# Four adaLN rows formed by GpSimd beside the latent attention, and a sixth early chunk pair in layer 0

## The chip, the cores and the metric

The kernel runs on one core of a Trainium2 chip. The metric is the device time of one execution in microseconds. Five engines work side by side, each with its own queue that is executed in order: TensorE (PE, matrix products), VectorE (DVE), ScalarE (ACT), GpSimd (POOL) and SyncE (SP, which here issues the transfers). An instruction that waits holds up everything behind it on its engine.

## The reference

A trunk of two layers on one sequence of 1024 tokens of width 1024, in float32. Each layer has a mixer of three head groups and a gated feed-forward part, and both are modulated by adaLN from a condition vector c:

```python
c_act = jax.nn.silu(c)
for l in range(DEPTH):
    mod = (c_act @ ada_w[l] + ada_b[l])[:, None, :]
    sh1, sc1, g1, sh2, sc2, g2 = jnp.split(mod, N_MOD, axis=-1)
    h = rms_norm(x, norm1_w[l]) * (1.0 + sc1) + sh1
    ...
    y = concat(window_attention(h), latent_attention(h), spatial_gating(h))   # shortened
    x = x + g1 * (group_norms(y) @ w_out[l])                                  # shortened
    h = rms_norm(x, norm2_w[l]) * (1.0 + sc2) + sh2
    x = x + g2 * ((silu(h @ w_gate) * (h @ w_up)) @ w_down[l])                # shortened
```

The six pieces of `mod` are the adaLN rows. In the kernel a row is named (layer, j), with j from 0 (sh1) to 5 (g2). Row (l, j) is the sum over 1024 entries of silu(c) times a row of 1024 columns of `ada_w`.

## The kernel before

**Stages.** Each layer runs as: projection of the input, window attention and spatial gating (layer 0 about 74 to 330 us of the profiled span, layer 1 1228 to 1500), latent attention with the output projection, which runs beside its second half (330 to 531, 1503 to 1706), the gate/up products (531 to 987, 1706 to 2142), and the down products (987 to 1205, 2141 to 2354).

**Precision and the product scheme.** Every float32 operand of a product is split into a high and a low part (`split`, L142 to L143 and L140: ACT casts the high part, DVE subtracts it from the operand to give the low one), and three products replace one (`mm3`, L134 to L137). The gate/up and down products are done in a seven-product scheme over pairs of chunks: `left` and `right` form sums of quarter blocks (L1435: POOL or DVE), each sum is split, and `gu_pair` (L1482) or the down stage multiplies them. There are 11 chunk pairs (NJ = 11) of seven steps each.

**adaLN rows.** A row is formed away from PE: the weights come in eight blocks of 128x1024 (the tile `ada`), and `ada_mac` (L253) multiplies block k by column k of `cact` (silu(c) as columns) and adds it to `acc`, all on DVE: L255 for the first block, L257 for the other seven. When all eight are in, `ada_reduce` (L401) transposes `acc` on PE, four blocks of 128x128 to one PSUM bank (L404, the tile `adaT`), and DVE sums the bank along its free dimension (L405, the tile `mc`); a whole row needs two such banks. `ada_finish` (L382) adds the bias and, for the rows that are needed along the free dimension, transposes and stores them to DRAM, from where `mod_row` (L473) loads them broadcast as `mrow`.

Three places make rows. `ada_rows_wide` (L407) runs as the step B of the order strings PRU0 and PRU1 in the projection stage, with two blocks at a step: rows (0,2), (0,4), (0,3) in layer 0 and (1,4), (1,3) in layer 1. `ada_bg` (L443) runs within the gate/up stage of layer 0, one block at a call, for the rows (0,5), (1,1), (1,0), (1,2) and (1,5). The first two rows of layer 0 are made at the start of the program, which the change doesn't touch.

**Early pairs.** `wd_early` (L1565) is run from within the gate/up stage: for each chunk pair j in EARLY[l] it loads two down-weight tiles (`dnr`, 128x1024), waits three steps, multiplies them by the gate row (L1575: one on DVE, one on POOL, with the row (l,5) as `mrow`), forms the seven right-hand sums, splits each (the tile `wpe`) and keeps it for a store to DRAM (`wp`). In the down stage such a pair's seven operands are loaded (`dnt<-wp`) and not formed. EARLY0[l] is the number of steps that pass first. Layer 0 has five early pairs and begins after 14 steps, layer 1 six and begins after one.

**What sets the order.** The kernel is written as generators, and strings of letters give the order of their steps: PRU0 and PRU1 in the projection stages, PRB0 and PRB1 in the latent attention, a letter for each generator (S the softmax, T and H the transposes of probabilities and heads, M the products with the values, O the output tiles, and so on; `sequences`, L197). In the gate/up stage `pair_steps` (L1697) calls `ahead(i)` before step i of a pair j > 0: it runs one step of `bg` (a multiply-add) if 7(j-1)+i < 9 or i < 4, then one step of `bg2` (the early pairs). Since an engine executes in program order, the place of a step in these strings is its place in each engine's queue.

**Names for the steps below.** `QK` holds queries and keys of one of eight sequence tiles; the rotation (L360 to L363, on POOL) is its last change, the copy L844 the one before; `qkTB` (L1160) are PE's transposes of them at the start of the latent attention, and `mB` (L1133, L1134) its mask. `pB`, `nmB` (L1177) are the masked scores and their negated maxima, `pTs` the split transposed probabilities. `ks`, `qs`, `kw`, `pLA`, `yA` belong to the window attention, `yc` to the spatial gating, `wor` to the output weights. Small tiles of 128x512 come from `AD` (L150), a pool of NAD = 4 buffers.

Of the kernel before, what the change touches and what calls it, by code (L numbers as in the profile page):

```python
# [12 lines left out]
ALU = mybir.AluOpType  # L13
AX = mybir.AxisListType

P = 128
# [37 lines left out]
DY1, DY2 = 0, 0  # L54
PRU0 = ("fKKRKKfKRKQKQSSKSKPPRBQVVRfKSPSSQLKKPRSPVVKPQVSPVKKSRPSLQVVKPSRPcSQcLRVVPLPQhShLcSSSVPVecczcVPPB"
       "hcPVVLVculuuxqzBBxLlueBxqoeuuLoeoqyosouuqlqylxxyxyysllohyBylsqxoqxyyBxxleyyxByyxyxyxooBysqxx")
PRU1 = ("fKfKKKfKRRKQKSSKQKPSPRSQVVSSKRKQLKPRPSPVVRPVKQoQSSSPVKKPVRSLBPVLKSQPVBcPcVRSQLBPeLVhcPhBSScVzSccB"
        "PVPcVhVVPBLcuuluozBxlLxeyquByquLxxllBoqouuuqosBeyllhoyyByllxxeyxBxqoyxxyyBoyxqxsyysBxqysxxeyyxqo")
PRB0 = ("HHHHSHHSSSHTTSTSTHTSTMMMMSTMHMTMSHTTMHSMMTTTMHTMMSMMMSTTSqHMSTMTHMTSqTMHTSMTMMMSMHTHTMTMTMMgTHMT"
       "MMSSSSTHSTMMHTwMqTTTMSMSMSTqTMTMHTTTMSMMHTMMMTSMSyxTSaMqSTTxHHMMSqxwMMSySxTSSTHyMHwSTMMSMyqTTMSM"  # L60
       "THaMOSSHTHMSHMqMMTTMSSqOSSTMqwMTTTMqSMMSSxwOMTyMyTyxxOMwOOqOnOnwOynbnbwOjbxObrnhOnkbhrsOssntttbt"
       "OtObbOtn")
PRB1 = ("HHHHSHHSSSHTTSTSTHTSTMMMMSTMHMTMSHTTMHSMMTTTMHTMMSMMMSTTSqHMSTMTHMTSqTMHTSMTMMMSMHTHTMTMTMMgTHMT"
       "MMSSSSTHSTMMHTwMqTTTMSMSMSTqTMTMHTTTMSMMHTMMMTSMSyxTSaMqSTTxHHMMSqxwMMSySxTSSTHyMHwSTMMSMyqTTMSM"
       "THaMOSSHTHMSHMqMMTTMSSqOSSTMqwMTTTMqSMMSSxwOMTyMyTyxxOMwOOqOnOnwOynbnbwOjbxObrnhOnkbhrsOssntttbt"
       "OtObbOtn")
EY = (1, 0, 1, 1, 0, 0, 0, 1)
ORD = ((0, 1, 2, 3, 4, 6, 5), (0, 2, 3, 1, 4, 6, 5))
AHEAD = (4, 2, 6, 10, 7, 9, 9)
EARLY = ((0, 1, 3, 5, 8), (0, 1, 3, 5, 6, 8))  # L70
EARLY0 = (14, 1)
NG = 33
NW = 12
NR = 4
# [5 lines left out]
def tile_trunk(ctx, tc, x, c, positions, ada_w, ada_b, norm1_w, w_in, a_sinks, b_q_norm_w, b_w_uq,  # L80
# [326 lines left out]
    def ada_rows_wide(l, js):  # L407
# [32 lines left out]
            yield  # L440
        drain(tail)

    def ada_bg(todo):  # L443

        steps = [(l, j, k) for l, j in todo for k in range(KD)]

        def load(l, j, k):
            raw = W([P, D], F32, "ada")
            DMA.dma_start(out=raw, in_=ada_w[l, k * P:(k + 1) * P, j * D:(j + 1) * D])
            return raw  # L450

        def finish(acc, mc, l, j):
            yield
            ada_reduce(acc[:, 0:512], mc[:, 0:4])
            ada_reduce(acc[:, 512:1024], mc[:, 4:8])
            yield from ada_finish(l, j, mc, 2)

        raw, tail = load(*steps[0]), iter(())
        for i, (l, j, k) in enumerate(steps):
            if k == 0:  # L460
                acc, mc = W([P, D], F32, "acc"), TN(8, "mc")
            cur = raw
            if i + 1 < len(steps):
                raw = load(*steps[i + 1])
            ada_mac(acc, cur, k)
            run(tail)
            yield
            if k == KD - 1:
                tail = finish(acc, mc, l, j)
        while run(tail):  # L470
            yield
# [82 lines left out]
    def layer(l, x_tiles):  # L554
# [5 lines left out]
        rs_kv = cst.tile([P, 8], F32, name=f"rskv{l}")  # L560
        rs_a = cst.tile([P, 8], F32, name=f"rsa{l}")
        rs_b = cst.tile([P, 8], F32, name=f"rsb{l}")
        bg = ada_rows_wide(l, (2, 4, 3) if l == 0 else (4, 3))


        w1, g1 = load_in_chunk(l, 512, 512, 2)
# [1099 lines left out]
        def build_t_seq():  # L1666
            need("b", 8)
            need("h", 2)
            b11, b12, b21, b22 = hb[0, 1], hb[0, 0], hb[1, 1], hb[1, 0]
            t2 = [G([P, 2, 512], F32, "t2") for _ in range(2)]  # L1670
            tt2(t2, b22, b12, ALU.subtract)
            yield
            split_h("t3", t2)
            yield
            tt2(t2, t2, b11, ALU.add)
            split_h("t2", t2)
            yield
# [12 lines left out]

        def prep_gu_seq():
            need("j", 1)
            for n in range(2):
                ready.append(next(gens[0]))
                yield

        def pair_steps(j):  # L1697
            def ahead(i):
                if j > 0:
                    if 7 * (j - 1) + i < 9 or i < 4:  # L1700
                        run(bg)
                    run(bg2)
                if i == 3 and j + 1 < NJ:
                    gens[j + 1] = gu_prep(load_gu(j + 1), ORD[1])
                want_gu(7 * j + (AHEAD[i] if j or i > 1 else 2))
            return gu_pair(j, lambda i: ready[7 * j + i], ahead)
# [10 lines left out]
        def pair_seq():  # L1717
            need("r", 2)
            yield from first_products(pair_steps(0), 6)

        seqs = dict(H=heads_seq(), S=soft_seq(), T=t_seq(), M=m_seq(), q=sq_seq(), a=ya_seq(), y=y_seq(), w=w_seq(),
                    g=g_seq(), x=x_seq(), O=o_seq(), k=mods_seq(), n=norm_seq(), b=hb_seq(), h=split_h_seq(),
                    t=build_t_seq(), j=load_gu_seq(), r=prep_gu_seq(), s=pair_seq())
        step, need = sequences(seqs)
        for k in (PRB0, PRB1)[l]:
            step(k)
        for k in seqs:
            need(k, 99)

        bg = ada_bg([(0, 5)] + [(1, j) for j in (1, 0, 2, 5)]) if l == 0 else iter(())  # L1730
        bg2 = wd_early()
        for j in range(1, NJ):
            g = pair_steps(j)
# [65 lines left out]
```

## Time and profile before

| | us |
|---|---|
| median of three runs | 2364.41 |
| lowest, highest | 2363.06, 2368.47 |
| the profiled execution's own time | 2363.91 |
| its span on the core | 2362.2 |
| mean granted clock of TensorE in it | 0.984 |

A row of a group gives line, engine, operation, what is written and read, shape and count, then the time busy in us with the mean of one in ns, then the engine's idle time just before and what ended it. A row of the timeline gives the start in us, the duration, and in square brackets how long the engine had been idle and what released it; "x8" in it joins neighbours of one kind. In a list of one tile's instructions stand the least, the median and the greatest duration in ns. PEld is the load of weights into the PE array, which overlaps the products.

### The profile page before, as it was taken

Reading aid. Unit: us, or ns where it says so; the run is one execution under the profiler, and the core shown is the slowest. Engines: PE = TensorE matmul, PEld = TensorE weight load, DVE = VectorE, ACT = ScalarE, POOL = GpSimd, SP = SyncE. Lnnn points to the kernel's source line nnn. Section 1 sums busy time; section 2 is a strip of 40 time slices with the busy share of each in tenths; the row PEclk is TensorE's granted clock in tenths of the full one; section 3 lists DMA queues with packets and bytes.
Section 4 is the critical chain, followed back from the end, with each engine's and each line's share of the span. In section 5 each row is a group of like instructions: output and inputs, shape, how many; then the busy total and the mean of one; then the engine's idle time right before and its main releaser. Section 6 shows DMA issues by size and latency. Waiting matters only on the chain. (4 is left out here: it accounts for less than half of the span.)

```text
span 2362.2 us, 31945 instructions
## 1 busy us (share of the span) xinstructions
PE 2253.7 (95%) x11191; PEld 1903.5 (81%) x11191; DVE 1783.3 (75%) x2793; ACT 1114.9 (47%) x2296; POOL 981.3 (42%) x997
## 2 busy tenths in 40 slices
PE   5899899999999999999999898999989999999998
PEld 4789798887888877878878787988878888888886
DVE  7787578848778777699974875688597676748978
ACT  4566377637334343323343653785464444432233
POOL 4666640322433323555554655202234243325643
PEclk9999999999999999999999999999999999999999
DMA  6503442212557465863240153222134545468433
GB/s 255 167 19 106 172 139 84 96 54 90 178 195 250 163 222 181 345 256 94 82 158 22 54 181 143 75 88 99 54 102 163 186 156 177 172 230 322 133 109 115
DMA packets 155397, 347.66 MB, mean 147 GB/s; under 512 B 12522, under 2 KB 71652, under 8 KB 155236
## 3 DMA queue, kind: packets, MB, share of 16 engines
q1 hardware_dynamic: 155236, 345.62, 41.9%
q8 instruction: 88, 1.44, 0.2%
q14 instruction: 73, 0.60, 0.1%
HBM read 250.65 MB, written 94.92 MB: 146 GB/s over the span
## 5 line engine op out<-in xcount | busy, mean ns | idle before, releaser
L140 DVE TENSOR_TENSOR gus<-gur,gus 128x512 fp32r<-128x512 f32 x264 | 230.8, 888 | 113.9 <-ACT gus L143 109.0
L135 PE MATMUL gate<-hTh,gus 128*128 128x512 f32 x616 | 244.2, 396 | 17.3 <-ACT u L1530 9.2
L143 ACT CAST gus<-gur 128x512 fp32r<-128x512 f32 x264 | 160.3, 624 | 197.0 <-DVE acc L257 53.4
L135 PE MATMUL down<-dnt,dns 128*128 128x512 f32 x616 | 240.9, 391 | 8.1 <-ACT dnt L143 6.8
L136 PE MATMUL gate<-hTl,gus 128*128 128x512 f32 x616 | 243.0, 394 | 0.6 <-DVE hTl L140 0.5
L137 PE MATMUL gate<-hTh,gus 128*128 128x512 f32 x616 | 242.4, 393 | 0.0
L135 PE MATMUL up<-hTh,gus 128*128 128x512 f32 x616 | 240.5, 390 | 1.6 <-ACT u L1530 1.6
L137 PE MATMUL down<-dnt,dns 128*128 128x512 f32 x616 | 240.0, 390 | 0.0
L136 PE MATMUL down<-dnt,dns 128*128 128x512 f32 x616 | 240.0, 390 | 0.0
L137 PE MATMUL up<-hTh,gus 128*128 128x512 f32 x616 | 239.9, 390 | 0.0
L136 PE MATMUL up<-hTl,gus 128*128 128x512 f32 x616 | 239.9, 389 | 0.0
L143 ACT CAST dns<-act 128x512 fp32r<-128x512 f32 x132 | 81.4, 621 | 234.4 <-PE down L137 178.2
L1435 POOL TENSOR_TENSOR gur<-gur 128x512 f32<-128x512 f32 x44 | 62.6, 1422 | 278.6 <-DVE gus L140 278.6
L1616 DVE TENSOR_TENSOR x<-x,down 128x512 f32<-128x512 f32 x224 | 147.5, 678 | 26.7 <-PE down L137 26.3
L135 PEld LDWEIGHTS gate<-hTh,gus 128*128 128x128 f32 x616 | 117.5, 191 | 43.6 <-ACT u L1530 10.0
L140 DVE TENSOR_TENSOR dns<-act,dns 128x512 fp32r<-128x512 f32 x132 | 136.3, 1050 | 13.0 <-ACT dns L143 13.0
L135 PEld LDWEIGHTS down<-dnt,dns 128*128 128x128 f32 x616 | 115.7, 188 | 35.5 <-ACT dnt L143 5.2
L1435 POOL TENSOR_TENSOR gur<-gur,s 128x512 f32<-128x512 f32 x44 | 67.5, 1540 | 181.1 <-DVE gus L140 181.1
L136 PEld LDWEIGHTS gate<-hTl,gus 128*128 128x128 f32 x616 | 117.5, 191 | 25.7 <-DVE hTl L140 1.7
L137 PEld LDWEIGHTS gate<-hTh,gus 128*128 128x128 f32 x616 | 117.2, 190 | 24.4
L135 PEld LDWEIGHTS up<-hTh,gus 128*128 128x128 f32 x616 | 115.8, 188 | 25.7 <-ACT u L1530 2.0
L136 PEld LDWEIGHTS up<-hTl,gus 128*128 128x128 f32 x616 | 115.7, 188 | 24.0
(417 smaller groups left out, 6209.5 us busy)
## 6 DMA issues: line engine op xcount, KB each, us to landing
gur<-in_w_gate_up_dram SPq DMA_DIRECT2D x88, 512.0 KB
ada<-in_ada_w_dram SPq DMA_DIRECT2D x80, 512.0 KB
wp<-wpe SPq DMA_DIRECT2D x77, 512.0 KB
dnt<-wp SPq DMA_DIRECT2D x77, 512.0 KB
dnr<-in_w_down_dram SPq DMA_DIRECT2D x44, 512.0 KB
act<-act SPq DMA_DIRECT2D x44, 512.0 KB
wr<-in_w_in_dram SPq DMA_DIRECT2D x24, 512.0 KB
x<-in_x_dram SPq DMA_DIRECT2D x16, 512.0 KB
```

The lines of the kernel that those rows point to most:

```text
L135: PE.matmul(ps, lh, rh, start=start, stop=False, skip_group_check=more)
L136: PE.matmul(ps, lh, rl, start=False, stop=False, skip_group_check=more)
L137: PE.matmul(ps, ll, rh, start=False, stop=stop, skip_group_check=more)
L140: eng.tensor_tensor(out=out_, in0=a, in1=b, op=ALU.subtract)
L143: ACT.copy(out=h, in_=src)
L1435: return lambda o, a, b, op: eng.tensor_tensor(out=o, in0=a, in1=b, op=op)
L1616: DVE.tensor_tensor(out=av_, in0=av_, in1=ps[t], op=ALU.add)
```

## The change

The rows (0,5), (1,1), (1,4) and (1,3) leave DVE and are formed on POOL during the latent attention: (0,5) and (1,1) in layer 0's, which were in the gate/up stage behind it, and (1,4) and (1,3) in layer 1's, which were in layer 1's projection. A new generator, `ada_half_rows`, makes each row in two halves of 512 columns. For each half there are eight loads of 128x512 (256 KB), eight multiplies by a column of `cact` and seven additions, as separate POOL instructions since the fused form of L257 is not used there; the half's `ada_reduce` then needs one PSUM bank. It is the step A in PRB0 and PRB1, 40 letters between the seventh and the 181st of the string. The 14 letters B of PRU1 go. In the gate/up stage of layer 0, `bg` keeps the rows (1,0), (1,2) and (1,5), and runs only at steps i < 4.

Chunk pair 6 joins the early pairs of layer 0, so that both layers have the pairs 0, 1, 3, 5, 6 and 8; layer 0's early work begins after three steps and not after 14. That is possible since the row (0,5), by which the down weights are multiplied, is then done before the stage begins.

By instruction counts: DVE loses 32 multiply-adds of 128x1024; POOL gains 64 multiplies and 56 additions of 128x512; SP issues 64 loads of 256 KB in place of 32 of 512 KB, and seven more stores and loads of `wp`. The seven right-hand operands of pair 6 move from the down stage (where POOL forms the sums and ACT and DVE split them) to the gate/up stage (where DVE forms the sums). PE's instructions are the same in number and kind.

```diff
-PRU1 = ("fKfKKKfKRRKQKSSKQKPSPRSQVVSSKRKQLKPRPSPVVRPVKQoQSSSPVKKPVRSLBPVLKSQPVBcPcVRSQLBPeLVhcPhBSScVzSccB"
+PRU1 = ("fKfKKKfKRRKQKSSKQKPSPRSQVVSSKRKQLKPRPSPVVRPVKQoQSSSPVKKPVRSLPVLKSQPVcPcVRSQLPeLVhcPhSScVzSccPVPcV"
...
-PRB0 = ("HHHHSHHSSSHTTSTSTHTSTMMMMSTMHMTMSHTTMHSMMTTTMHTMMSMMMSTTSqHMSTMTHMTSqTMHTSMTMMMSMHTHTMTMTMMgTHMT"
+PRB0 = ("HHHHSHAHSSASHTTASTSATHTSATMMAMMSTAMHMATMSHATTMAHSMMATTTAMHTMAMSMAMMSTATSqAHMSTAMTHAMTSqATMHATSMTA"
...
+PROWS = ([(0, 5), (1, 1)], [(1, 4), (1, 3)])
+GROWS = [(1, j) for j in (0, 2, 5)]
-EARLY = ((0, 1, 3, 5, 8), (0, 1, 3, 5, 6, 8))
-EARLY0 = (14, 1)
+EARLY = ((0, 1, 3, 5, 6, 8), (0, 1, 3, 5, 6, 8))
+EARLY0 = (3, 1)
...
+    def ada_half_rows(todo):
+
+        steps = [(l, j, hf, k) for l, j in todo for hf in range(2) for k in range(KD)]
+
+        def load(l, j, hf, k):
+            raw = AD("ada")
+            DMA.dma_start(out=raw, in_=ada_w[l, k * P:(k + 1) * P, j * D + hf * 512:j * D + hf * 512 + 512])
+            return raw
+
+        raw, tail = load(*steps[0]), iter(())
+        yield
+        for i, (l, j, hf, k) in enumerate(steps):
+            if k == 0:
+                acc = AD("acc")
+                mc = TN(8, "mc") if hf == 0 else mc
+            cur = raw
+            if i + 1 < len(steps):
+                raw = load(*steps[i + 1])
+            col = cact[:, k:k + 1]
+            if k == 0:
+                POOL.tensor_scalar(out=acc, in0=cur, scalar1=col, scalar2=None, op0=ALU.mult)
+            else:
+                POOL.tensor_scalar(out=cur, in0=cur, scalar1=col, scalar2=None, op0=ALU.mult)
+                POOL.tensor_tensor(out=acc, in0=acc, in1=cur, op=ALU.add)
+            run(tail)
+            yield
+            if k == KD - 1:
+                def finish(acc, mc, l, j, hf):
+                    yield
+                    ada_reduce(acc, mc[:, 4 * hf:4 * hf + 4])
+                    yield
+                    if hf:
+                        yield from ada_finish(l, j, mc, 2)
...
-        bg = ada_rows_wide(l, (2, 4, 3) if l == 0 else (4, 3))
+        bg = ada_rows_wide(0, (2, 4, 3)) if l == 0 else iter(())
+        bgp = ada_half_rows(PROWS[l])
...
-                    if 7 * (j - 1) + i < 9 or i < 4:
+                    if i < 4:
                         run(bg)
...
-                    t=build_t_seq(), j=load_gu_seq(), r=prep_gu_seq(), s=pair_seq())
+                    t=build_t_seq(), j=load_gu_seq(), r=prep_gu_seq(), s=pair_seq(), A=bgp)
...
-        bg = ada_bg([(0, 5)] + [(1, j) for j in (1, 0, 2, 5)]) if l == 0 else iter(())
+        bg = ada_bg(GROWS) if l == 0 else iter(())
```

What the change does to the engines' queues is shown at three places. Line numbers of the changed kernel are higher: by 2 up to the new function, by 43 behind it (L360 becomes L362, L844 becomes L887). The new POOL lines are L465 (the first multiply, into `acc`), L467 (the other multiplies) and L468 (the additions).

First place: POOL's queue at the end of layer 0's projection, where the last of the eight `QK` tiles is rotated and the mask is written. Before:

```order
L844 COPY QK_3820<-ckv_2694 128x2x32
L360 TENSOR_TENSOR r_778_3853<-QK_3820,cost 128x192
L361 TENSOR_TENSOR r_779_3854<-QK_3820,sint 128x192
L362 TENSOR_TENSOR QK_3820<-r_778_3853,r_779_3854 128x6x16
L363 TENSOR_TENSOR QK_3820<-r_778_3853,r_779_3854 128x6x16
L1133 MEMSET mB_3915 128x896
L1134 COPY mB_3915<-maskA 128x128
L1099 TENSOR_TENSOR wor_5441<-wor_5441,mrow_944_4549 128x512
```

Now, from the same copy of the last tile's rotary keys:

```order
L887 COPY QK_3827<-ckv_2701 128x2x32
L465 TENSOR_SCALAR acc_4015<-ada_3984,cact 128x512
L468 TENSOR_TENSOR acc_4015<-acc_4015,ada_4017 128x512
L467 TENSOR_SCALAR ada_4056<-ada_4056,cact 128x512
L468 TENSOR_TENSOR acc_4015<-acc_4015,ada_4056 128x512
L362 TENSOR_TENSOR r_778_3860<-QK_3827,cost 128x192
L363 TENSOR_TENSOR r_779_3861<-QK_3827,sint 128x192
L467 TENSOR_SCALAR ada_4091<-ada_4091,cact 128x512
L364 TENSOR_TENSOR QK_3827<-r_778_3860,r_779_3861 128x6x16
L365 TENSOR_TENSOR QK_3827<-r_778_3860,r_779_3861 128x6x16
L1176 MEMSET mB_3922 128x896
L1177 COPY mB_3922<-maskA 128x128
```

One multiply, one addition, a multiply and an addition of the first half row stand between the copy and the rotation, a third multiply within the rotation, and the mask and the output weights come later than these.

Second place: DVE's queue in layer 1's projection, ahead of the casts of a key tile of the window attention. Before:

```order
L255 TENSOR_SCALAR acc_12847<-ada_12722,cact 128x1024
L858 CAST qs_12958<-qk_12773 128x6x64
L257 SCALAR_TENSOR_TENSOR acc_12847<-ada_12724,cact,acc_12847 128x1024
L140 TENSOR_TENSOR qs_12958<-qk_12773,qs_12958 128x6x64
L873 CAST qva_12986<-av_11350 128x2x64
L888 CAST kw_13004<-kw_12819 128x4x128
L140 TENSOR_TENSOR qva_12986<-av_11350,qva_12986 128x2x64
L257 SCALAR_TENSOR_TENSOR acc_12847<-ada_12849,cact,acc_12847 128x1024
L140 TENSOR_TENSOR pLA_12895<-pTA_12896,pHA_12894 128x384
L140 TENSOR_TENSOR pLA_12895<-pTA_12902,pHA_12894 128x384
L943 TENSOR_TENSOR yA_12843<-avA_12946,tmpA_12951 64x128 x3
L864 CAST ks_12961<-qk_12773 128x128 x2
```

Now:

```order
L901 CAST qs_13052<-qk_12875 128x6x64
L916 CAST qva_13080<-av_11456 128x2x64
L142 TENSOR_TENSOR qs_13052<-qk_12875,qs_13052 128x6x64
L142 TENSOR_TENSOR qva_13080<-av_11456,qva_13080 128x2x64
L931 CAST kw_13098<-kw_12921 128x4x128
L142 TENSOR_TENSOR pLA_12989<-pTA_12990,pHA_12988 128x384
L142 TENSOR_TENSOR pLA_12989<-pTA_12996,pHA_12988 128x384
L986 TENSOR_TENSOR yA_12945<-avA_13040,tmpA_13045 64x128 x3
L907 CAST ks_13055<-qk_12875 128x128 x2
```

The three multiply-adds, L255 and twice L257, are gone from the stretch; the rest stands in nearly the same order.

Third place: DVE's queue in layer 0's latent attention, where the first half row is summed along its bank. Before:

```order
L140 TENSOR_TENSOR kTl_3921<-qkTB_4210,kTh_3920 64x512
L1177 ISA pB_4217,nmB_4225<-sB_4218,mB_3915 128x768
L1177 ISA nmB_4225 128x1
L140 TENSOR_TENSOR pTs_4238<-pTB_4233,pTs_4238 128x512
L140 TENSOR_TENSOR pTs_4246<-pTB_4241,pTs_4246 128x512
L140 TENSOR_TENSOR pTs_4254<-pTB_4249,pTs_4254 128x512
L140 TENSOR_TENSOR qT_4177<-qkTB_4259,qT_4177 96x512
```

Now:

```order
L142 TENSOR_TENSOR kTl_3928<-qkTB_4256,kTh_3927 64x512
L1220 ISA pB_4263,nmB_4271<-sB_4264,mB_3922 128x768
L1220 ISA nmB_4271 128x1
L407 TENSOR_REDUCE mc_4016<-adaT_4283 128x4
L142 TENSOR_TENSOR pTs_4294<-pTB_4289,pTs_4294 128x512
L142 TENSOR_TENSOR pTs_4302<-pTB_4297,pTs_4302 128x512
L142 TENSOR_TENSOR pTs_4310<-pTB_4305,pTs_4310 128x512
L142 TENSOR_TENSOR qT_4215<-qkTB_4319,qT_4215 96x512
```

The sum `mc` of the bank `adaT` stands behind the masked maximum of a score tile and ahead of three splits of probabilities.

More of the change, by code (lines that the diff above doesn't have):

```diff
@@ L56 @@
        "hcPVVLVculuuxqzBBxLlueBxqoeuuLoeoqyosouuqlqylxxyxyysllohyBylsqxoqxyyBxxleyyxByyxyxyxooBysqxx")
-PRU1 = ("fKfKKKfKRRKQKSSKQKPSPRSQVVSSKRKQLKPRPSPVVRPVKQoQSSSPVKKPVRSLBPVLKSQPVBcPcVRSQLBPeLVhcPhBSScVzSccB"
-        "PVPcVhVVPBLcuuluozBxlLxeyquByquLxxllBoqouuuqosBeyllhoyyByllxxeyxBxqoyxxyyBoyxqxsyysBxqysxxeyyxqo")
-PRB0 = ("HHHHSHHSSSHTTSTSTHTSTMMMMSTMHMTMSHTTMHSMMTTTMHTMMSMMMSTTSqHMSTMTHMTSqTMHTSMTMMMSMHTHTMTMTMMgTHMT"
[L60 to L66, printed above, removed]
+PRU1 = ("fKfKKKfKRRKQKSSKQKPSPRSQVVSSKRKQLKPRPSPVVRPVKQoQSSSPVKKPVRSLPVLKSQPVcPcVRSQLPeLVhcPhSScVzSccPVPcV"
+        "hVVPLcuuluozxlLxeyquyquLxxlloqouuuqoseyllhoyyyllxxeyxxqoyxxyyoyxqxsyysxqysxxeyyxqo")
+PRB0 = ("HHHHSHAHSSASHTTASTSATHTSATMMAMMSTAMHMATMSHATTMAHSMMATTTAMHTMAMSMAMMSTATSqAHMSTAMTHAMTSqATMHATSMTA"
+        "MMMASMHTAHTMATMTMAMgTAHMTMAMSSASSTHASTMAMHTwAMqTATTMSAMSMASTqTAMTMAHTTTAMSMAMHTMAMMTASMSyxTSaMqST"
+        "TxHHMMSqxwMMSySxTSSTHyMHwSTMMSMyqTTMSMTHaMOSSHTHMSHMqMMTTMSSqOSSTMqwMTTTMqSMMSSxwOMTyMyTyxxOMwOOq"
+        "OnOnwOynbnbwOjbxObrnhOnkbhrsOssntttbtOtObbOtn")
+PRB1 = ("HHHHSHAHSSASHTTASTSATHTSATMMAMMSTAMHMATMSHATTMAHSMMATTTAMHTMAMSMAMMSTATSqAHMSTAMTHAMTSqATMHATSMTA"
+        "MMMASMHTAHTMATMTMAMgTAHMTMAMSSASSTHASTMAMHTwAMqTATTMSAMSMASTqTAMTMAHTTTAMSMAMHTMAMMTASMSyxTSaMqST"
+        "TxHHMMSqxwMMSySxTSSTHyMHwSTMMSMyqTTMSMTHaMOSSHTHMSHMqMMTTMSSqOSSTMqwMTTTMqSMMSSxwOMTyMyTyxxOMwOOq"
+        "OnOnwOynbnbwOjbxObrnhOnkbhrsOssntttbtOtObbOtn")
+PROWS = ([(0, 5), (1, 1)], [(1, 4), (1, 3)])
+GROWS = [(1, j) for j in (0, 2, 5)]
 EY = (1, 0, 1, 1, 0, 0, 0, 1)
@@ L441, in ada_rows_wide @@
         drain(tail)
+    def ada_half_rows(todo):
[28 more added lines that the diff above has]
+                        yield from ada_finish(l, j, mc, 2)
+                while run(tail):
+                    yield
+                tail = finish(acc, mc, l, j, hf)
+        while run(tail):
+            yield
     def ada_bg(todo):
```

## The prediction, made before the changed kernel was run

> **What bounds the kernel now.** I read the page's busy shares first, then a table of busy time by stage, then the waits of TensorE.
>
> ```profile
> span 2362.2 us, 31945 instructions
> PE 2253.7 (95%) x11191; PEld 1903.5 (81%) x11191; DVE 1783.3 (75%) x2793; ACT 1114.9 (47%) x2296; POOL 981.3 (42%) x997
> ```
>
> TensorE (PE) is busy for 95% of the span, and both kernels issue the same matrix products. So a change can only win what PE loses now: idle gaps, about 108 us in all, and time at a lower granted clock. GpSimd (POOL) is busy for 42%, but the share of a whole run says nothing of one stage. The table by stage does. In its rows stand the window, its length, then busy time (and instructions) of PE, PE's weight loads, DVE, ACT and POOL, the granted clock, and the share and rate of the DMA engines.
>
> ```profile
> 531.30:987.30 456.00, 439.80 (x1945) 361.96 (x1943) 352.44 (x417) 191.88 (x353) 156.15 (x101) 0.98 0.57 197
> 1705.90:2141.60 435.70, 429.75 (x1900) 355.34 (x1899) 311.16 (x373) 200.54 (x356) 156.34 (x104) 1.00 0.49 171
> 987.10:1204.80 217.70, 211.37 (x928) 173.28 (x927) 197.03 (x233) 71.69 (x123) 120.98 (x74) 1.00 0.46 161
> 2141.40:2353.70 212.30, 210.48 (x925) 173.12 (x923) 183.39 (x228) 68.34 (x118) 103.90 (x72) 1.00 0.45 161
> 1228.00:1500.00 272.00, 253.66 (x1455) 225.83 (x1453) 165.56 (x398) 135.56 (x359) 152.74 (x235) 0.96 0.28 91
> 330.00:531.00 201.00, 200.69 (x1162) 171.87 (x1161) 152.01 (x289) 125.48 (x265) 38.55 (x37) 1.00 0.22 80
> ```
>
> The rows are, from the top: the gate/up stage of layer 0 and of layer 1, the down stage of layer 0 and of layer 1, the projection stage of layer 1, and the latent attention with the output projection of layer 0. Layer 1 does the same gate/up and down work as layer 0, with six early chunk pairs and no adaLN rows beside it, and takes 20.3 and 5.4 us less. In the latent attention PE has no idle time worth naming (0.3 of 201 us), POOL works only 38.6 us, and DVE 152. That is where the change puts its work: onto an idle engine, but beside the one stage in which PE never waits.
>
> ```profile
> PE gate L135 <- ACT u L1530: 9.2, 2, 5.4
> PE down L135 <- ACT dnt L143: 6.8, 5, 1.6
> ```
>
> These are rows of PE's waits (total us, times, longest). The first belongs to two stalls in layer 0's gate/up stage, of 5.4 and, by difference, 3.8 us; the second mostly to the operands of the down stage, split only when they are needed.
>
> **What leaves layer 1's projection.** Sixteen multiply-adds of 128x1024 (eight make an adaLN row, and two rows go) leave DVE's queue there.
>
> ```profile
> L257 DVE SCALAR_TENSOR_TENSOR acc<-ada,cact,acc 128x1024 f32<-128x1024 f32 x70 | 98.6, 1408 | 26.4 <-DMA ada<-in_ada_w_dram 26.2
> 1355.39 1.27 DVE L257 SCALAR_TENSOR_TENSOR acc<-ada,cact,acc 128x1024 f32<-128x1024 f32 x1
> 1358.52 0.36 DVE L864 CAST ks<-qk 128x128 fp32r<-128x128 f32 x2
> 1358.90 0.30 PE L884 MATMUL kT<-ident,ks 128*128 128x128 f32 x1 [2.92 <-DVE ks L864]
> 1360.00:1366.80 6.80, 6.80 (x31) 6.80 (x30) 4.92 (x14) 3.28 (x10) 3.91 (x5) 0.50 0.80 244
> ```
>
> At 1358.90 PE had stood idle for 2.92 us for the keys that DVE casts at 1358.52. Ahead of that cast three multiply-adds stand within eight rows (the order block on DVE), 1.27 us the last, so some 3.7 us of queue go, more than the wait: I count all 2.9 as won. Right behind the stall 6.8 us run at half the clock, which costs 3.4; I count that too, since the clock is full ahead of the stall and whole again soon after. Next late there is the transpose of the queries on PE itself, which is no wait.
>
> ```profile
> 1460.67 1.04 PE L404 MATMUL adaT<-ident,acc 128*128 128x128 f32 x8
> 1464.54 0.41 PE L812 MATMUL lowT<-ident,ckv 128*128 128x128 f32 x2 [0.91 <-DVE yc L630]
> 1466.32 0.41 PE L135 MATMUL ukv<-uph,lowk 128*128 128x384 f32 x1 [1.36 <-DVE yc L630]
> 1469.06 1.28 DVE L405 TENSOR_REDUCE mc<-adaT 128x4 f32<-128x512 f32 x2
> ```
>
> The eight transposes that end a row fill two PSUM banks at 1460.67, and these are free only when DVE reduces them at 1469.06. Between the two PE waits 0.91 and 1.36 us; I count these 2.3 us as a lack of banks. The transposes themselves, 1.04 us a row, go with two rows: 2.1. Sum of this stage: 2.9 + 3.4 + 2.3 + 2.1 = **10.7 us** won. If only the transposes and the bank waits go it is 4.4, which is its lower end.
>
> **What leaves layer 0's gate/up stage.** Of 40 multiply-adds 24 stay, four in each of the pairs 1 to 6, and pairs 7 to 10 have none. In return one more chunk pair's down operands are loaded, multiplied, split and stored here, seven splits more, and that work begins at step 3 instead of 14.
>
> ```profile
> L449 SPq DMA_DIRECT2D ada<-in_ada_w_dram x40: 328/384/1189, 585.3 to 921.5; - x40
> 840.48 2.66 POOL L1575 TENSOR_TENSOR dnr<-dnr,mrow 128x1024 f32<-128x1024 f32 x1 [10.29 <-DMA dnr<-in_w_down_dram]
> 846.90 0.79 PE L135 MATMUL gate<-hTh,gus 128*128 128x512 f32 x1 [5.38 <-ACT u L1530]
> 844.50:851.30 6.80, 4.39 (x10) 3.46 (x11) 5.77 (x7) 3.02 (x6) 4.05 (x3) 0.50 0.69 204
> ```
>
> The 5.4 us stall began with a load of down weights that came late: POOL could not multiply until 840.48, ACT's split of that product stood at the head of ACT's queue and the copies that free PSUM behind it, and PE waited. With 5.4 us goes 3.4 of half clock. Two readings: both big stalls lie in pairs 7 to 10 (the row's loads run to 921.5), where no multiply-add is left, so both go; or they come wherever early work and adaLN loads run together, which is now the case in pairs 1 to 6, and they only change places. By the first 14.3 us go (5.4 + 3.4 + 3.8, and 1.7 estimated for the second stall's clock), by the second nothing; these are the ends. Between them I take the stage's excess over layer 1, which has all six early pairs and no row: 20.3 us for 40 multiply-adds and their transposes, and 16/40 of it, **8.1 us**.
>
> **Layer 0's down stage** gets the same six ready pairs as layer 1's. Its idle time is 217.70 - 211.37 = 6.3 us against 212.30 - 210.48 = 1.8, so **4.5 us** go; between 3 and the whole 5.4.
>
> **What comes into the latent attention.** Each half row is 8 multiplies by a column and 7 adds of 128x512 on POOL. The trace has POOL's two-input form of that shape, but not the one-input form.
>
> ```profile
> L844 POOL COPY QK<-ckv x16: 232/236/245, 232.4 to 1495.6; 128x64 f32<-128x64 f32 x16
> L1134 POOL COPY mB<-maskA x2: 289/290/290, 326.3 to 1500.7; 128x128 f32<-128x128 f32 x2
> L1099 POOL TENSOR_TENSOR wor<-wor,mrow x16: 1278/1292/2301, 332.2 to 1628.5; 128x512 f32<-128x512 f32 x16
> 1621.16 3.23 SPq L1248 DMA_DIRECT2D wor<-in_w_out_dram  x3
> 1623.91 3.54 POOL L1099 TENSOR_TENSOR wor<-wor,mrow 128x512 f32<-128x512 f32 x2 [3.70 <-DMA wor<-in_w_out_dram]
> ```
>
> From 0.236 to 0.290 us for 64 more columns, 512 columns make about 0.61; the bounds are 0.29 and the two-input form's 1.29. I take 0.6, since a copy is also a one-input operation. A half row is then 8 x 0.6 + 7 x 1.29 = 13.8 us, and at most 19.4 if a multiply costs 1.29. A 256 KB load issued at 1621.16 fed POOL at 1623.91: 2.75 us, hidden while two or more raw tiles are ahead.
>
> *Pace.* PE's transposes of the four half rows of layer 0 stand, in the changed order, at the work that ran at 351.71 for the first and 399.63 for the last.
>
> ```profile
> 351.71 1.04 PE L1196 MATMUL pTB<-ident,pB 128*128 128x128 f32 x8
> 399.63 0.36 PE L1220 MATMUL avB<-pTs,vB 128*128 128x256 f32 x1
> L1255 ACT CAST yTh<-y32a x4: 1037/1042/1048, 413.8 to 1636.5; 128x1024 fp32r<-128x1024 f32 x4
> ```
>
> POOL ends the first half row at about 340 (below), and three more by 340 + 3 x 13.8 = 381. It has 18 us to spare. The loads of the output weights, of x and of y32a now queue on SP behind these 32 loads; POOL's last load frees SP near 380, and y32a, the first that is needed, is read at 413.8.
>
> *Start.* The order block on POOL shows four operations of the half row ahead of the last tile's rotation, and a fifth within it.
>
> ```profile
> 321.41 0.24 POOL L844 COPY QK<-ckv 128x64 f32<-128x64 f32 x1
> 325.14 0.39 POOL L363 TENSOR_TENSOR QK<-r,r 128x96 f32<-128x96 f32 x1
> 326.77 1.71 PE L1160 MATMUL qkTB<-ident,QK 128*96 128x128 f32 x14 [0.45 <-DVE mc L405]
> 1499.63 0.39 POOL L363 TENSOR_TENSOR QK<-r,r 128x96 f32<-128x96 f32 x1
> 1500.95 2.43 PE L1160 MATMUL qkTB<-ident,QK 128*96 128x128 f32 x18 [1.42 <-DVE vB L851]
> ```
>
> From 321.65, the end of the copy, a multiply (0.6) and an add (1.29) bring POOL to 323.5. The next multiply needs a load that waits for the first multiply's tile: 322.25 + 2.75 = 325.0. With it and its add POOL is at 326.9, and the rotation, some 2.2 us with the gaps, with one multiply within it, ends at about 329.8 instead of 325.5. PE wants the last tile at its twelfth transpose, the eighth of the 14 from 326.77, so at 327.6: a stall of 2.2 us. In layer 1 the rotation ended at 1500.02; 4.3 us later, less some 0.8 that POOL idled there, is 1503.5, and the twelfth of the 18 from 1500.95 stands at 1502.4: 1.1 us. Behind the 5.4 us stall the clock was halved for 6.8 us; behind these shorter ones I take half of that, a loss of 1.7 each. Start: 2.2 + 1.1 + 3.4 = **6.7 us** lost; without the clock 3.3, and with multiplies of 1.29 and the full half clock 15.
>
> *In the stage.* Eight half rows bring four transposes each: half of 1.04, **4.2 us**. Each holds one PSUM bank until DVE's reduce, whose place the third order block shows behind a softmax maximum. The one wait of this sort in the trace is the 0.45 us of the row at 326.77. Eight of them make **3.6**; the ends are 0 and, with a reduce of 0.64 us waited for in full, 8 x 1.1 = 8.8.
>
> **The sum**: won 10.7 + 8.1 + 4.5 = 23.3, lost 6.7 + 4.2 + 3.6 = 14.5, net 8.8. Stalls that all go are an upper reading of layer 1's part, so I give 1.5 back: 7.3. The profiled execution took 2363.9 us (its span and 1.7 around it), 0.5 under the median of the runs. Forecast: **2356.6 us**.
>
> **Rivals.**
> 1. *The gate/up stage gives nothing back.* The stalls there come from late loads, not from DVE's load alone; seven more steps bring seven more loads, stores and splits. For it: the 5.4 us stall released by a down weight. Against it: layer 1 runs the same six pairs with 1.00 clock. Time: 2356.6 + 8.1 = 2364.7, no change.
> 2. *POOL doesn't keep pace* and PE waits for its sums (slower). By the places above this decides once a half row costs over (399.6 - 340) / 3 = 19.9 us. The slowest two-input operation in the row of L1099 took 2.30; with that and multiplies of 1.29 a half row is 26.4 us, the last sum is 20 us late in each layer, and the time is about 2397. Against it: the median of that row is 1.29.
>
> ```profile
> 840.24 0.69 DVE L140 TENSOR_TENSOR gus<-gur,gus 128x512 fp32r<-128x512 f32 x1
> ```
>
> The Trainium skill ("GPSIMD Engine Reference", section 4.1 Engine selection) speaks against the move: element-wise work with two inputs belongs on VectorE, GpSimd being about twice as slow. The trace agrees (1.29 us against 0.69). By that rule alone the sums would come late wherever POOL has no room, which is this rival, so it keeps a chance although its room of 18 us is ample by the rows.
>
> 3. *POOL slows DVE in this stage* (slower).
>
> ```profile
> L140 DVE TENSOR_TENSOR dns<-act,dns 128x512 fp32r<-128x512 f32 x132 | 136.3, 1050 | 13.0 <-ACT dns L143 13.0
> L140 DVE TENSOR_TENSOR pTs<-pTB,pTs 128x512 fp32r<-128x512 f32 (+1 forms) x120 | 73.3, 630 | 11.0 <-ACT pTs L1199 10.1
> ```
>
> In the down stages DVE's subtraction of two SBUF tiles takes 1.05 us, with POOL busy half of the time; the split of the probabilities, which reads PSUM, takes 0.63 in the latent attention. If the latter rose to the former, 60 in a layer cost 25 us of DVE, of which half is hidden in its 49 idle us: 12 a layer, 2381. [...]
> 4. *More goes than counted*: both gate/up stalls vanish (6.2 more) and the start costs no clock (3.4): 2347.
> 5. *The change does not move the work* is out: the order shows 120 new POOL rows and 32 fewer on DVE.
>
> **How the numbers follow.** Forecast 0.50, rival 1 0.22, rival 2 0.07, rival 3 0.11, rival 4 0.10. The predicted time is 2356.6. Down from it, rival 4 with no bank wait reaches 2343; up, nothing from the gate/up stage with a start of 15 reaches 2373, and rival 3 with five sixths of its 24 us 2377: the range is 2343 to 2377, which leaves out rival 2 and the end of rival 3. A measurement here tells 0.2%, 4.7 us, from no change, so faster is below 2359.7. Of the forecast's 0.50 I put 0.38 there, with rival 4 that makes 0.48; the rest of it and most of rival 1 are within, 0.29; slower 0.23.
>
> **What would show it.** Right: layer 1's projection near 1355 without a wait for ks; PE idle 2 to 3 us at the first latent transposes of both layers, with a wait for POOL's QK; the latent attention longer by 5 to 9 us in each layer; POOL's multiply near 0.6; the layer 0 down stage near 213. Wrong: waits of PE for POOL's acc inside the latent attention (rival 2), pTs well over 0.63 (rival 3), a gate/up stage of layer 0 still at 456 (rival 1).

## The result, and the profile after

The changed kernel is slower: 2395.28 us (median of four runs, 2392.80 to 2400.71) against 2366.44 us for the kernel before beside it; the ratio is 1.0126, with a 95% interval from 1.0113 to 1.0140. The profiled execution of the changed kernel took 2400.71 us, the slowest of its four, so that the spans below differ by 36.7 us and the medians by 28.8.

The busy shares on the page of the profile after:

```profile
PE 2268.0 (95%) x11191; PEld 1909.1 (80%) x11191; DVE 1738.3 (72%) x2765; ACT 1120.2 (47%) x2296; POOL 1132.6 (47%) x1113
```

POOL works 151 us more and DVE 45 less. The table by stage of the profile after, in the same columns as before: the gate/up stage of layer 0, then the latent attention of layer 0 and of layer 1, from the first `qkTB` to the last scores.

```profile
564.00:1013.30 449.30, 437.40 (x1927) 359.97 (x1926) 339.75 (x406) 196.43 (x359) 161.55 (x103) 0.98 0.55 193
326.00:482.50 156.50, 136.18 (x824) 115.70 (x824) 116.34 (x238) 100.36 (x209) 103.39 (x78) 0.91 0.37 124
1507.80:1660.50 152.70, 134.90 (x821) 114.82 (x822) 115.57 (x236) 99.84 (x207) 103.49 (x78) 0.92 0.37 126
```

The stage that had no idle time to speak of now idles for 20.3 and 17.8 us and runs at a mean clock of 0.91 and 0.92. PE's waits say for whom:

```profile
PE adaT L406 <- POOL acc L468: 22.8, 4, 8.9
PE qkTB L1203 <- POOL QK L365: 11.5, 2, 6.7
PE gate L137 <- ACT u L1573: 4.9, 2, 3.8
PE down L137 <- ACT dnt L145: 3.1, 2, 1.5
PE kT L927 <- DVE ks L907: 1.1, 2, 0.9
```

The first two rows are new, and both name POOL: its sums of the half rows, and the rotated last tile behind the first half row. The other three are rows of before, shrunk: 9.2 to 4.9, 6.8 to 3.1, and, for the keys, 3.2 to 1.1.

By stages, each measured from its first product (`qkTB`, `gate`, `down`) to the next stage's, in us, with the runs that are told below:

| | before | after | mul_by_tt | spread | spread_y32a | tt_late_spread | mul_as_copy |
|---|---|---|---|---|---|---|---|
| latent attention 0 | 205.5 | 238.0 | 221.8 | 230.2 | 223.8 | 213.1 | 218.7 |
| gate/up 0 | 455.9 | 449.3 | 448.4 | 447.4 | 450.2 | 447.1 | 451.3 |
| down 0 | 217.3 | 212.4 | 212.1 | 212.5 | 212.1 | 212.3 | 212.1 |
| projection 1 | 296.5 | 282.1 | 280.3 | 278.7 | 281.0 | 279.5 | 280.4 |
| latent attention 1 | 204.9 | 233.6 | 217.3 | 228.5 | 222.1 | 209.3 | 214.7 |

After against before: 6.6 + 4.9 + 14.4 = 25.9 us won, 32.5 + 28.7 = 61.2 lost in the latent attentions, and 1.4 in the rest, which makes the 36.7 of the spans. Each column is one execution, and executions of one kernel lie up to 12 us apart (mul_as_copy: 2352.45 to 2364.87), so a column's net is less sure than the medians. The gains are there. What the rows cost on POOL is the whole question.

The timeline of POOL and PE at layer 0's first half row, and at its last sum:

```profile
323.76 0.24 POOL L887 COPY QK<-ckv 128x64 f32<-128x64 f32 x1
323.98 1.56 POOL L465 TENSOR_SCALAR acc<-ada,cact 128x512 f32<-128x512 f32 x1
325.63 1.27 POOL L468 TENSOR_TENSOR acc<-acc,ada 128x512 f32<-128x512 f32 x1
328.38 1.56 POOL L467 TENSOR_SCALAR ada<-ada,cact 128x512 f32<-128x512 f32 x1 [1.48 <-DMA ada<-in_ada_w_dram]
...
334.23 0.39 POOL L365 TENSOR_TENSOR QK<-r,r 128x96 f32<-128x96 f32 x1
334.68 0.88 PE L1203 MATMUL qkTB<-ident,QK 128*96 128x128 f32 x3 [6.65 <-POOL QK L365]
...
424.32 1.26 POOL L468 TENSOR_TENSOR acc<-acc,ada 128x512 f32<-128x512 f32 x1
425.63 1.12 PE L406 MATMUL adaT<-ident,acc 128*128 128x128 f32 x4 [8.85 <-POOL acc L468]
```

A multiply takes 1.56 us, not 0.6, and is dearer than the two-input add (1.27, or 1.28 in the mean). The rotated tile is ready at 334.6 and PE has waited 6.65 us; the last sum of the layer comes 8.85 us late. Three windows of the table by stage, around the three waits of this layer, show the granted clock halved, partly while PE idles:

```profile
329.20:339.40 10.20, 4.72 (x20) 4.54 (x21) 2.06 (x3) 2.88 (x5) 10.03 (x12) 0.51 0.42 131
397.50:400.90 3.40, 3.30 (x14) 2.94 (x15) 1.93 (x3) 0.58 (x1) 0.05 (x1) 0.51 0.27 78
418.00:431.70 13.70, 6.07 (x26) 5.30 (x27) 4.09 (x6) 1.75 (x3) 11.21 (x10) 0.50 0.53 172
```

### The profile page after: what moved, and what is told of

The parts are those of the page before. It is cut to its first block, busy times and chain, and to the rows that moved or that the text cites. A ratio compares the mean times of both kernels' runs of the same rounds, so it can differ in the third digit from the quotient of the medians.

```text
span 2398.9 us, 32119 instructions
## 1 busy us (share of the span) xinstructions
PE 2268.0 (95%) x11191; PEld 1909.1 (80%) x11191; DVE 1738.3 (72%) x2765; ACT 1120.2 (47%) x2296; POOL 1132.6 (47%) x1113
```

## The experiments

The theory after this reading (A): POOL's own time for a half row, 8 x 1.56 + 7 x 1.28 = 21.4 us and waits for loads, lies above the 16 to 20 us between PE's places for the sums (from the rows of the prediction's pace: (399.63 - 351.71) / 3 = 16.0, and 19.9 with the room ahead of the first), so PE runs at POOL's pace. Against it stood: the loads set the pace (B); the start is the costly part (C); POOL's work slows DVE or takes PE's banks wherever it stands (D).

**mul_by_tt.** The multiplies as two-input products with the column broadcast (the first of a half row, into `acc`, likewise, here and in the runs below):

```diff
-                POOL.tensor_scalar(out=cur, in0=cur, scalar1=col, scalar2=None, op0=ALU.mult)
+                POOL.tensor_tensor(out=cur, in0=cur, in1=col.to_broadcast([P, 512]), op=ALU.mult)
```

> The multiplies of the half rows as two-input products with the column broadcast, nothing else changed. Theory A (POOL's own time for a half row, 8 x 1.56 + 7 x 1.28 = 21.4 us and the waits for loads, sets the pace, and PE waits for the sums): a product of 1.28 us saves 2.2 us in each half row, and the last of four sums comes some 7 to 9 us earlier in each layer; time 2375 to 2384. Rival B (the loads set the pace, POOL waits 26.6 us for them): POOL waits longer by what it saves, time 2390 or more. If the broadcast product itself takes 1.56 or more, neither is told apart.

Measured: 2364.42 us, ratio to the kernel before 0.9999 (0.9988 to 1.0010): the whole loss of 29 us against before is gone by this one form. The time lies below the expected 2375 to 2384, as the product took 1.05 us and not 1.28. Its group of products on POOL:

```profile
L467 POOL TENSOR_TENSOR ada<-ada,cact 128x512 f32<-128x512 f32 x56 | 58.7, 1049 | 31.1 <-DMA ada<-in_ada_w_dram 29.1 <-PE uq L139 1.7
```

And PE's one wait for POOL in this stage:

```profile
PE qkTB L1203 <- POOL QK L365: 6.0, 2, 3.6
```

No wait for `acc` is left. The last sum of layer 0 is just in time:

```profile
407.55 1.28 POOL L468 TENSOR_TENSOR acc<-acc,ada 128x512 f32<-128x512 f32 x1
409.91 0.60 PE L406 MATMUL adaT<-ident,acc 128*128 128x128 f32 x4
```

1.05 us makes a half row 17.4 us of POOL's own work. From the first multiply to the last add of layer 0's four half rows POOL took 86.8 us, waits included, where the changed kernel took 101.6; the sum is ready at 408.8, about 1 us before PE takes it. POOL still waits 29.1 us for loads, no less than in the changed kernel (26.6), while 31 us are gained, so B is out as the cause.

**start_late.** The first three loads of the half rows wait for the mask (`late` gives the tile `mB`):

```diff
             raw = AD("ada")
+            if (l, j, hf, k) in steps[:3]:
+                after(raw, late())
```

> The first three loads of the half rows wait until the mask has been begun, so that no operation of a half row stands ahead of the last tile's rotation; PE's order is unchanged. Theory A: the start wait (6.7 and 4.8 us for the rotated tile) goes, but POOL begins later and PE reaches the sums earlier, so the waits for acc grow by nearly as much; time 2384 to 2396. Rival C (the start is the costly part, the waits for acc follow from it): 2365 to 2375.

Measured: 2394.43 us, ratio 1.0123 (1.0103 to 1.0143), no gain; theory A had 2384 to 2396.

```profile
PE adaT L406 <- POOL acc L470: 28.5, 8, 5.7
```

The wait for the rotated tile is gone, and PE waits at all eight sums instead of four, 28.5 us instead of 22.8. POOL's waits for loads of these multiplies fell from 26.6 to 8.9 us without any gain, which speaks against B once more. C falls: taking away a wait in front of a queue that is too slow only moves the wait.

**spread.** As start_late, with the 40 letters A placed so that five other letters stand between one and the next (layer 1's string likewise):

```diff
-PRB0 = ("HHHHSHAHSSASHTTASTSATHTSATMMAMMSTAMHMATMSHATTMAHSMMATTTAMHTMAMSMAMMSTATSqAHMSTAMTHAMTSqATMHATSMTA"
+PRB0 = ("HHHHSHHSSSHTTSATSTHTASTMMMAMSTMHAMTMSHATTMHSAMMTTTAMHTMMASMMMSATTSqHAMSTMTAHMTSqATMHTSAMTMMMASMHT"
...
```

> The same work with the same instructions, begun after the mask, and the 40 steps placed every fifth letter, so that PE reaches the four sums some 15 to 23 us later than before. Theory A: no wait for POOL is left, and with it the half clock behind the waits; of the 61 us lost in the two latent attentions some 50 come back; time 2335 to 2350, faster than the kernel before. Rival D (POOL's work beside the attention slows DVE or takes PE's banks wherever it stands): at least half of the loss stays, time 2370 or more.

Measured: 2384.57 us, ratio 1.0084 (1.0067 to 1.0101). No wait for a sum was left, but the time missed the expectation by over 30 us and lies where rival D put it. The timeline of PE, ACT and SP around the stall of layer 0, from its end back:

```profile
438.30 0.64 PE L1205 MATMUL qkTB<-ident,QK 128*64 128x128 f32 x2 [16.87 <-DVE tmpB L1279]
435.87 1.04 ACT L1300 CAST yTh<-y32a 128x1024 fp32r<-128x1024 f32 x1 [17.59 <-DMA y32a<-ya]
429.91 0.38 SPq L1378 DMA_DIRECT2D y32a<-ya  x1
426.13 3.21 SPq L1293 DMA_DIRECT2D wor<-in_w_out_dram  x2
```

ACT's wait for both layers, in the list of its waits:

```profile
ACT yTh L1300 <- DMA y32a<-ya: 35.5, 2, 18.0
```

PE waits for DVE, DVE for a copy of ACT, and ACT for the load of `y32a`, which SP issued at 429.91 and not at 342.4 as before. On SP it stands behind loads of `wor` and of half rows, which wait for POOL to free their buffers (in SP's waits from 320 to 445 us, 56.9 us of the half rows' loads are for POOL's adds). POOL's pace had reached PE by another way, through SP's queue.

**spread_y32a.** One letter `a` of each layer's string, that load, moved ahead to the ninth place, before the first A.

> The kernel of the run named spread, with one letter moved: the load of the first y32a stands at the eighth letter, ahead of the loads of the half rows on SP. In spread it was issued at 429.9 us, behind loads that waited for POOL's buffers; ACT waited 17.6 us for it and PE 16.9 us at 421.4, and again in layer 1. Theory F (that one load is what spread lost): both waits and the 17 us of half clock behind each go; 2384 less 34 and less 17, so 2333 to 2345. Rival G (another load or engine is as late behind it): over 2360.

Measured: 2374.27 us, ratio 1.0029 (1.0019 to 1.0040): 10 us gained of the 40 to 50 expected, as rival G has it (over 2360).

```profile
PE oAB L137 <- DMA wo<-wo: 9.0, 2, 5.0
PE adaT L406 <- POOL acc L470: 7.7, 2, 4.4
```

Theory F was only part of it: both stalls of 17 us are gone, but with `y32a` early the last sums of each layer are late again, and the next load in SP's queue, that of the output weights, is late behind the same POOL. The expectation also took the clock for too much: in the two halved windows of spread, 17.1 us each, PE was busy for only 3.5 and 3.7 us, so they cost under 4 us together and not 17; in this run the halved stretches of the two stages hold 18.7 us of PE's work, which cost 9. With the multiply at 1.56 us neither of the two spacings that were tried hides the four half rows; whether another does is open.

**mul_on_act.** The multiplies as scaled copies on ACT:

```diff
-                POOL.tensor_scalar(out=cur, in0=cur, scalar1=col, scalar2=None, op0=ALU.mult)
+                ACT.activation(out=cur, in_=cur, func=AF.Identity, scale=col)
```

> The multiplies go to ACT (as a scaled copy, some 0.6 to 0.7 us), POOL keeps the seven adds. POOL needs 9 us for a half row. Theory A: no wait for sums is left; the start wait shrinks to under 3 us; time 2345 to 2365. Rival E (ACT's queue waits for late loads and holds up the softmax): waits of PE for ACT appear, time 2380 or more.

Measured: 2380.71 us, ratio 1.0065 (1.0045 to 1.0085). That is rival E (2380 or more). In PE's waits the softmax on ACT stands where POOL's sums stood:

```profile
PE pTB L1239 <- ACT pB L1223: 10.2, 11, 1.5
PE avB L1263 <- ACT pTs L1242: 4.7, 7, 1.9
```

ACT itself waits for the half rows' loads, and the group of POOL's adds has its idle time behind ACT's multiplies:

```profile
ACT ada L467 <- DMA ada<-in_ada_w_dram: 16.7, 20, 2.0
L468 POOL TENSOR_TENSOR acc<-acc,ada 128x512 f32<-128x512 f32 x56 | 71.8, 1282 | 88.5 <-ACT ada L467 69.4 <-DVE pTs L142 11.4 <-DVE qT L142 3.9
```

No wait of PE for sums is left; the multiplies now hold up ACT's own work and POOL. Some 5 us more are lost ahead of the stage, whose first `qkTB` runs at 330.7 us and not at 325.7 as before.

**pool_forms.** A price list: another operation for each block of a half row.

> A price list of POOL operations on 128x512 in place of the multiplies of the half rows (blocks 2 to 5 of each half: a multiply by a constant, a copy, a product with the column broadcast, a product with acc; blocks 6 and 7: the multiply by a column on 256 and on 128 columns only), so the four rows hold other values than the reference's. If the multiply-by-column form is dear for each element, 256 columns take about 0.8 and 128 about 0.45 us, and the multiply by a constant also takes 1.56. If the column operand is what costs, the constant takes 0.5 to 0.7, as the copy does by my extrapolation (0.61). Time is of no interest; some 2370.

The groups of POOL's operations, by form; mean ns of one behind the comma:

```profile
L465 POOL TENSOR_SCALAR acc<-ada,cact 128x512 f32<-128x512 f32 x8 | 12.5, 1567 | 0.2
L468 POOL TENSOR_SCALAR ada<-ada,cact 128x512 f32<-128x512 f32 x8 | 13.0, 1626 | 16.3 <-DMA ada<-in_ada_w_dram 16.3
L470 POOL TENSOR_SCALAR ada<-ada 128x512 f32<-128x512 f32 x8 | 11.9, 1492 | 8.1 <-DMA ada<-in_ada_w_dram 8.1
L476 POOL TENSOR_TENSOR ada<-ada,acc 128x512 f32<-128x512 f32 x8 | 10.3, 1286 | 1.6 <-DMA ada<-in_ada_w_dram 1.1
L474 POOL TENSOR_TENSOR ada<-ada,cact 128x512 f32<-128x512 f32 x8 | 8.3, 1042 | 4.7 <-DMA ada<-in_ada_w_dram 4.7
L478 POOL TENSOR_SCALAR ada<-ada,cact 128x256 f32<-128x256 f32 x8 | 7.4, 926 | 0.5 <-DMA ada<-in_ada_w_dram 0.2
L472 POOL COPY ada<-ada 128x512 f32<-128x512 f32 x8 | 4.9, 613 | 0.0
L480 POOL TENSOR_SCALAR ada<-ada,cact 128x128 f32<-128x128 f32 x8 | 4.8, 606 | 2.1 <-DMA ada<-in_ada_w_dram 2.1
```

A copy takes 0.613 us; the multiply by a constant 1.49 (expected 1.56), by a column 1.57 (one of the eight of L468 took 2.02, which lifts their mean), and by a column on 256 and 128 columns 0.926 and 0.606 (expected 0.8 and 0.45). So the form is dear and not the column operand: 0.606, 0.926 and 1.567 us for 128, 256 and 512 columns make 0.32 us for the first 128 more and 0.32 for each 128 after that, about 2.5 ns a column on a base of 0.3 us. A product with a full second operand takes 1.29, with a broadcast one 1.04. The one run took 2371.59 us; its half row costs POOL 18.1 us by these prices, and the time stands between that of mul_by_tt (17.4 us, 2364.42) and that of the changed kernel (21.4 us, 2395.28).

**mul_as_copy.** The changed kernel with `POOL.tensor_copy` in place of the multiplies, which has the price that the prediction summed with; it leaves out the column factors:

```diff
-                POOL.tensor_scalar(out=cur, in0=cur, scalar1=col, scalar2=None, op0=ALU.mult)
+                POOL.tensor_copy(out=cur, in_=cur)
```

> The changed kernel with each multiply of the half rows replaced by a POOL copy (0.61 us in pool_forms), so the column factors are left out of the four rows. This is the kernel that the prediction summed. Theory A (the price of the multiply is the only step that failed): no wait of PE for acc, the start wait is 2 to 4 us a layer, and the time lies at the prediction's 2356.6 within 6 us. Rival H (loads, the start or the banks would have cost as much with the cheap multiply too): 2364 or more, as mul_by_tt, or waits for acc stay.

Measured: 2358.80 us, ratio 0.9970 (0.9958 to 0.9983); the prediction said 2356.6. PE's wait for the rotated tile:

```profile
PE qkTB L1203 <- POOL QK L365: 3.8, 2, 2.6
```

No wait for `acc` is left, and the start waits are 2.6 and, by difference, 1.2 us, where the prediction had 2.2 and 1.1 (the second lies under the 2 to 4 expected here). So the price was what brought the late sums and the long start waits, and the time comes within 2.2 us of the forecast. The terms don't all come out. By the table, the latent attentions lose 13.2 + 9.8 = 23.0 us, where the prediction had 14.5, and the other stages win 4.6 + 5.2 + 16.1 = 25.9, where it had 23.3; this execution, of 2362.01 us, is 1.9 below that of before, while the medians differ by 6.9. That the time agrees so closely is in part luck. One row in the latent attention that neither the profile before nor the prediction has:

```profile
PE pTB L1239 <- ACT pB L1223: 3.3, 4, 1.4
```

The changed kernel has it too. What holds up the softmax there, and what else makes up the 8.5 us, no run tells.

**tt_late_spread.** The kernel of spread_y32a with the broadcast products of mul_by_tt.

> Broadcast products (1.05 us), begun after the mask, every fifth letter, y32a's load moved ahead. Theory A with F: no wait for sums, for the rotated tile or for y32a is left; what stays of the change in the latent attention is the transposes and the reduces, some 3 to 5 us in each layer. Against the kernel before: 26 us won in the other stages, 6 to 10 lost; 2345 to 2352. It should be equal to spread_y32a within 5 us, since with room on POOL the multiply's price no longer counts. Rival: POOL's price counts anyway (2355 or more for spread_y32a, less here).

Measured: 2350.01 us (2345.42 to 2354.11), ratio 0.9934 (0.9914 to 0.9953): faster than before and than the change. Its two latent attentions:

```profile
329.00:475.00 146.00, 141.90 (x894) 122.18 (x893) 130.47 (x259) 106.35 (x221) 95.12 (x80) 1.00 0.45 152
1476.00:1620.00 144.00, 140.80 (x894) 121.19 (x895) 125.63 (x261) 107.81 (x222) 94.20 (x81) 1.00 0.46 158
```

The clock is whole, and PE idles 3 to 4 us. The time is 24 us under that of spread_y32a, which differs only in the form of the multiply: the expectation that the two would be equal was wrong, its rival right. Rival D falls with this run: POOL does as many operations beside the attention, and the two stages are only 7.6 and 4.4 us longer than before.

**tt_five_pairs** and **tt_late_five.** mul_by_tt and tt_late_spread with the early pairs of before, and with their later start:

```diff
-EARLY = ((0, 1, 3, 5, 6, 8), (0, 1, 3, 5, 6, 8))
-EARLY0 = (3, 1)
+EARLY = ((0, 1, 3, 5, 8), (0, 1, 3, 5, 6, 8))
+EARLY0 = (14, 1)
```

> The kernel of mul_by_tt with the five early pairs of before in layer 0, begun after 14 steps. If the sixth pair is what brings the down stage's 5 us, that stage is 217 us again and the gate/up stage as now (449) or shorter by up to 3; time 2364 to 2370. Rival: the down stage stays at 212 (then the moved rows did it), time 2360 to 2364.

> tt_late_spread with the five early pairs of before in layer 0. The sixth pair took 5 us from the down stage where the whole change was made, but in tt_five_pairs that stage was 215.1 without it, and the gate/up stage 3.3 shorter. If the sixth pair brings nothing: equal to tt_late_spread (2350) within 3 us, with the down stage some 3 longer and the gate/up stage some 3 shorter. If it brings its 4.5 us: 2354 or more.

Measured: 2362.95 us, ratio 0.9984 (0.9969 to 0.9998), and 2349.13 us, ratio 0.9926 (0.9909 to 0.9943). Without the sixth pair the down stage of layer 0 takes 215.1 and 218.1 us (212.1 and 212.3 with it), and the gate/up stage 445.1 and 442.1 (448.4 and 447.1 with it). The 217 or 212 us expected for the down stage of tt_five_pairs are both missed: of the 4.9 us won there, 2.2 stay without the sixth pair, and none in tt_late_five; no run tells why the two differ. What the sixth pair with its earlier start takes from one stage it adds to the other, and no change of the time is clear of the noise: the ratios with and without it, 0.9999 and 0.9984, 0.9934 and 0.9926, have overlapping intervals.

## Why the prediction was wrong

**The step that failed** is the price of POOL's multiply: "From 0.236 to 0.290 us for 64 more columns, 512 columns make about 0.61; the bounds are 0.29 and the two-input form's 1.29. I take 0.6, since a copy is also a one-input operation." The extrapolation of the copy was right to the last digit (0.613), but the operation is not a copy: it took 1.56 us, above the upper bound too. That bound rests on the assumption that one input can't cost more than two. The trace of before could not have given the price. It has the multiply's own form, TENSOR_SCALAR, on POOL only with 1 or 4 columns, and a one-input operation of another form with 512, which the prediction overlooked and which would have spoken for 0.6 just the same:

```profile
L172 POOL TENSOR_SCALAR ms<-sskv 128x1 f32<-128x1 f32 x16 | 3.1, 194 | 1.3
L533 POOL TENSOR_SCALAR_AFFINE_SELECT ws<-ws 128x512 f32<-128x512 f32 x2 | 1.3, 640 | 0.1
```

A half row was thus 21.4 us of POOL's own work, which alone is above the 19.9 at which the prediction's rival 2 decides. A second term was put at nothing: the loads, "hidden while two or more raw tiles are ahead". POOL waited 26.6 us for them, 3.3 in each half row, which makes 24.7. With copies these waits were 37.7 us; the last sum of layer 0 was ready at 399.1 us and PE took it at 408.2, so the room was 9 us and not 18. There the term cost PE nothing.

Rival 2 was there with the right mechanism and the right point, and had a chance of 0.07 because its price was bounded by rows of other operations. That its 2397 us lies so near the measured 2395 is luck: it has the adds dear (2.30) and the multiplies at 1.29, and puts all the loss on a last sum 20 us late in each layer. Measured were 22.8 us of waits for sums in both layers together, 11.5 for the rotated tiles, and the half clock.

**The start** (forecast 2.2 and 1.1 us of wait) was 6.65 and 4.82 by the same price: three multiplies stand ahead of the last rotation and within it. The sum also left out one that stands ahead of the rotation before it:

```profile
319.86 2.01 POOL L467 TENSOR_SCALAR ada<-ada,cact 128x512 f32<-128x512 f32 x1 [2.62 <-PE ukv L139]
```

The copy from which the sum starts ended at 324.0 us and not at 321.65. With copies the waits were 2.6 and 1.2.

**The half clock** was put at 1.7 us a layer, for the start alone; the waits for sums added more of it. In layer 0 PE was busy 4.72 + 3.30 + 6.07 = 14.1 us in the three halved windows, which cost 7 us, and in layer 1's three 12.9 us, which cost 6.5.

**What held.** Layer 1's projection won 14.4 us (forecast 10.7), though the wait for the keys did not go whole: 0.9 of its 2.9 us stayed. Layer 0's gate/up stage won 6.6 (8.1). Its two big stalls, in pairs 7 to 10, are gone, and one of 3.8 us stands 275 us into the stage, where 1.6 stood before: each of the prediction's two readings is right in part. The down stage won 4.9 (4.5). Sum 25.9 against 23.3. But the 4.9 are not a net gain: by the runs with five pairs the sixth pair and its earlier start cost 3 to 5 us in the gate/up stage, for which the sum, with its 16/40 of layer 1's advantage, had no term.

**Rival 3**, DVE slowed by POOL, did not come. The group of the probabilities' split after:

```profile
L142 DVE TENSOR_TENSOR pTs<-pTB,pTs 128x512 fp32r<-128x512 f32 (+1 forms) x120 | 73.4, 630 | 10.8 <-ACT pTs L1242 10.0
```

The mean was 630 ns before and is 630 now, with POOL busy for 103.4 of 156.5 us of the stage. The Trainium skill ("SBUF — State Buffer", section Who interferes with whom) has it that a DVE instruction with at most one SBUF input does not contend with GpSimd, as long as it is not in a 2-port mode. The trace agrees: of the split's two inputs one lies in PSUM.

**The cover on SP's queue** ("POOL's last load frees SP near 380, and y32a, the first that is needed, is read at 413.8") was gone too: the changed kernel issues that load at 435.0 us. No wait of ACT for it is listed there, where PE was late already; in spread, with the load at 429.9, it cost two stalls of 17 us.

## What to carry to other kernels

The price of an operation that the trace doesn't show can be bounded only by rows of its own form, not by a form that seems heavier; where the plan stands on a single such price, one small run that times a few forms settles it. When work moves to an idle engine, compare its time for a unit with the distance between the places at which the consumer takes the units, and look at every queue that waits for buffers of that engine: a late producer here showed up first as a late sum, and then, when the sums were given room, as a late load of other data. Here, removing the first wait of a chain that was too slow only moved the wait. And a total that agrees with the forecast proves little until its terms are compared one by one.

## What the runs showed of the hardware that was not expected

On POOL, in the half rows of these runs, for 128x512 float32: a multiply by a scalar took 1.49 to 1.57 us but for single slower ones, the add or product of two tiles 1.28 to 1.29, a product whose second operand is one column broadcast 1.04 to 1.05, and a copy 0.61. The multiply with one input was thus the dearest of them. These prices are not fixed: two-input rows of that shape in the gate/up stages of the kernel before took 1.42 to 1.65 us in the mean (L1435), for a reason that no run shows. The Trainium skill ("GPSIMD Engine Reference", section 4.1 Engine selection) has it that GpSimd's one-input work is roughly at line rate. That may fit the copy, at under half the price of the two-input add; it does not fit the multiply, at 1.2 times that price, and the measurement decides.
